# Output projection in two sets of banks, a fixed queue for the second norm, attention outputs scaled once per pair of heads

## The chip, the cores and the metric

The kernel runs on one core of a Trainium2 chip. The metric is device time in microseconds (us) of one execution. TensorE multiplies matrices, VectorE and ScalarE work element by element, GpSimd (POOL) does small operations and issues some DMAs, SyncE (SP) issues most of the others.

## The reference, cut to what matters

One layer over 1,024 frames of width 1,024: a norm, an input projection, two attentions (A in a band of chunks, B over keys that a top-k search selects), a gated recurrence C, a sigmoid-gated merge of the three, an output projection added to x, a second norm, a SwiGLU FFN added to x.

```python
h = rms_norm(x, g_mix[l])
z = h @ w_in[l]
...
p = jax.nn.softmax(sc, axis=-1).astype(v.dtype)
o = jnp.einsum('bhcqk,bckhd->bcqhd', p, vb)
...
merged = (gates[:, :, 0] * (y_a @ wb[:A_WIDTH])
          + gates[:, :, 1] * (y_b @ wb[A_WIDTH:A_WIDTH + B_WIDTH])
          + gates[:, :, 2] * (y_c @ wb[A_WIDTH + B_WIDTH:]))
x = x + merged @ w_out[l]
gu = rms_norm(x, g_ffn[l]) @ w_ffn_in[l]
g_, u_ = jnp.split(gu, 2, axis=-1)
x = x + (jax.nn.silu(g_) * u_) @ w_ffn_out[l]
```

## The kernel before

Every large product is made of three passes (`mm3`, L116 to L119): each operand is split into a high half, made by ScalarE (L101), and a low half, the rest, made by VectorE (L102), and high x high, high x low and low x high are added up in one bank of PSUM. The large products also go by a scheme with seven products of quarter matrices instead of eight, so that sums and differences of quarters have to be formed on VectorE before the splits and the results added after.

Instructions of each engine run in a fixed order. It is made when the program is built: a planner with a model of the durations takes, for each engine, the instruction that is ready by its model and stands first in the program. Loads on SP that are marked stay in program order. Buffers are slots of an arena with first-in first-out lists (`Slots`, L55); an instruction that writes a slot waits for the last reader of what was in it.

The stages, in the order of time: input norm and index scores (to some 90 us), then a long mixed stretch to some 620 us, in which the string `ORDER` (L38) interleaves the steps of attention A, the top-k search K, the gates G, C, attention B and others; the gates' rest to 670 us; the merge of the three branches to 788 us (L950 to L983); the output projection (L1081 to L1105); the second norm and the first FFN product (L1106 to L1110, L1217 to L1219); the FFN input part to some 1,310 us, the FFN output part to the end.

Attention (L396): for a pair of heads `pr`, a block `i` of 128 queries and each head `e`, `dots` puts scores into a bank S, L406 subtracts the maximum (VectorE), L409 takes the exp with its sum (ScalarE), L411 takes the reciprocal of the sum and L412 scales P (both VectorE), L418 transposes P (TensorE), L419 copies it back (ScalarE); L426 multiplies by v for both heads, L428 copies the result to 128 columns of `yT`. After the eighth block the pair's `yT` is stored to DRAM (L446 for A, L749 for B); it is loaded again in the merge.

Output projection (L958 to L1105): the merged M is kept in quarters; A11, A12, A21, A22 are quarters of M (two tiles each), b11 to b22 quarters of the weights, loaded by `load_wo` (b22 and b21 last). `o_prep(n)` forms the operands of product n and splits them; `order` (L1071) says which product comes when: 1, 5, 6, 4, 7, 2, 3. Each has four row tiles t of 12 matmuls of 512 columns, 48 in all. Products 1, 6 and 7 pile up in the banks X (0 to 3), the others have banks 4 to 7. `adds` (L1069) says into which half rows h and half columns of x2 each is added, with which sign (L1099).

Second norm (L993): for each of four row tiles a square with its sum (L997, ScalarE), a reciprocal root on POOL (L126, L127), a scaling (L999, VectorE), and a store of x2 (L1000). `evac2` transposes (L1016) and copies out (L1017). The norm of the upper rows and its splits (`trans2_first`) come after product 7, two products before the end; that of the lower rows after the last. Then `trans2_second` (L1032) forms the differences of quarters (L1039 to L1042) and splits them. `ffn_first(j)` makes two products of 12 matmuls with the quarters 11 and 21 of the upper rows alone; `ffn_rest(j)` makes the other five and needs T2, T1, T3, 22 and T4, in this order.

Of the kernel before, what the change touches and what calls it, by code (L numbers as in the profile page):

```python
# [10 lines left out]
F32 = mybir.dt.float32  # L11
# [68 lines left out]
def hybrid_kernel(ctx: ExitStack, tc: tile.TileContext, x, xt, small, cs, bias_a, lru_w, w_idx, w_zg, w_c, w_g, w_b,  # L80
# [315 lines left out]
    def attention(i, b0, pr, qk, v, mask, yT, isB=False):  # L396
# [4 lines left out]
        for e in range(2):  # L401
# [28 lines left out]

    def steps_A():
        for pr in range(2):
# [5 lines left out]
            yA = sl.get((128, T), F32, "yA")  # L438
            qk = to_stack(zA[pr], ga8, smc("ga", 1))
            for i in range(NT):  # L440
                b0 = max(0, i - 4)
                w = (i + 1 - b0) * 128
                attention(i, b0, pr, qk, vA, lambda h: bA[h % 2][:, 640 - w:640], yA)
# [296 lines left out]
    def steps_B():  # L740
        for pr in range(2):
            yB = sl.get((128, T), F32, "yB")
            qk = to_stack(zB[pr], None, None)
            for i in range(NT):
                w = (i + 1) * 128
                mk = mask[i] if i >= 2 else m01[:, 256 - w:256]
                attention(i, 0, pr, qk, vB, lambda h: mk, yB, True)
                if i == NT - 1:
                    nc.gpsimd.dma_start(y_dram[2 + pr], yB)  # L749
# [200 lines left out]
    for ot in range(8):  # L950
# [42 lines left out]
    def norm2(g):  # L993
        xn = []
        for t in range(4 * g, 4 * g + 4):
# [3 lines left out]
            V.tensor_scalar(j, x2[t], rs2[:, t:t + 1], None, op0=OP.mult)  # L999
# [20 lines left out]
    def keep(name, g, raw):  # L1020
        hb_[name, g] = (sl.get((128, 2, 512), F32R, "hh"), sl.get((128, 2, 512), F32R, "hl"))
        split(raw, *hb_[name, g])
# [8 lines left out]

    def trans2_second(xn, raws):  # L1032
        pairs = [(evac2(xn, g), evac2(xn, 2 + g)) for g in range(2)]
        sl.free(*xn)
        for g in range(2):
            b11, b21 = raws[g], raws[2 + g]
            b12, b22 = pairs[g]
            t2 = sl.get((128, 2, 512), F32, "t2")
            V.tensor_sub(b11, b12, b11)  # L1039
            V.tensor_tensor(b12, b22, b12, op=OP.subtract)  # L1040
            V.tensor_sub(t2, b22, b11)
            V.tensor_tensor(b21, b21, t2, op=OP.subtract)  # L1042
            for name, r in (("T2", t2), ("T3", b12), ("T1", b11), ("22", b22), ("T4", b21)):
                keep(name, g, r)
                sl.free(r)

    b22, b21 = load_wo(3), load_wo(2)
    A12, A21, A22 = ([M[kp + d][h] for kp in range(2)] for h, d in ((1, 2), (0, 0), (0, 2)))
    ss = [sl.get((128, 2, 512), F32, "s") for _ in range(2)]

    def o_prep(n):
        if n == "5":
            comb(ss, A21, OP.add, A22)
        elif n == "6":
            comb(ts, b22, OP.subtract, ts)
            comb(ss, ss, OP.subtract, A11)
        elif n == "4":
            comb(ts, ts, OP.subtract, b21)
# [3 lines left out]
        elif n == "3":  # L1062
            comb(ss, A12, OP.subtract, ss)
        r = o_split(*{"5": (ss, ts), "6": (ss, ts), "4": (A22, ts), "7": (A21, b12), "2": (A12, b21), "3": (ss, b22)}[n])
        for f in {"4": (A22, ts), "7": (A11, A21, b12), "3": (A12, ss, b21, b22)}.get(n, ()):
# [15 lines left out]
    for s_, n in enumerate(order):  # L1081
# [393 lines left out]
```

## Time and profile before

| | us |
|---|---|
| median of 3 runs | 1525.81 (1522.98 to 1526.56) |
| the profiled execution | 1523.58 |
| its span, first to last instruction | 1521.8 |
| TensorE busy | 1468.5 |
| VectorE busy | 1127.9 |
| ScalarE busy | 760.0 |

A busy share is an average over stages with different limits. Matmuls are pipelined, so each shows a duration of about 0.39 us while they start 0.23 us apart; the count of matmuls in a stretch says more than the busy time. PEclk is the clock granted to TensorE as a share of its full 2.4 GHz. A bracket at the end of an instruction's row gives the idle time of its engine before it and what ended that.

### The profile page before, as it was taken

To read this page: it belongs to the slowest core of one execution; us is meant where nothing else is said; L and a number is where in the kernel's file an instruction comes from. 1 tells how busy PE (TensorE), PEld (TensorE's weight loads), DVE (VectorE), ACT (ScalarE), POOL (GpSimd) and SP (SyncE) were. 2 spreads that over 40 slices of the span, in tenths; PEclk is the share of its full clock that TensorE was granted. 3 is DMA by queue.
4 is the path that set the end of the run, shared out by engine and by line. 5 is a ranking of instruction groups with operands and counts; after the bars stand their busy time and mean duration, and the time that the engine had idled before them with its cause. 6 is when DMAs were issued, how large, how long until landed. Compare 5 with 4: busy or idle time off the path is not lost.

```text
span 1521.8 us, 19934 instructions
## 1 busy us (share of the span) xinstructions
PE 1468.5 (96%) x7556; PEld 1227.0 (81%) x7556; DVE 1127.9 (74%) x1997; ACT 760.0 (50%) x1204; POOL 109.3 (7%) x161
## 2 busy tenths in 40 slices
PE   6999899999999998999998989999999999999999
PEld 5897688989788886788886868888888888888887
DVE  7889999869666779767889785555555556478872
ACT  6557768865778666443114563333333333344440
POOL 2220011210000200110000200000000000000000
PEclk9999999999999999999999999999999999999999
DMA  7011213112111121448461322323232323597532
GB/s 287 28 46 56 83 32 111 31 68 84 56 56 42 59 95 42 139 166 332 179 209 55 124 83 98 111 97 111 97 111 98 111 97 125 220 387 265 192 124 90
DMA packets 52241, 182.59 MB, mean 120 GB/s; under 512 B 6001, under 2 KB 6129, under 8 KB 52145
## 3 DMA queue, kind: packets, MB, share of 16 engines
q1 hardware_dynamic: 38448, 135.17, 25.8%
q0 software_dynamic: 11968, 43.00, 7.2%
q10 hardware_dynamic: 1728, 3.15, 0.5%
q8 instruction: 59, 0.97, 0.3%
q14 instruction: 38, 0.30, 0.1%
HBM read 135.94 MB, written 45.35 MB: 119 GB/s over the span
## 4 chain that ended last, share of the span: by engine, by line
PE 76%; DVE 17%; ACT 4%; issue 2%; DMA 1%; ACTq 0%; DVEq 0%; SPq 0%
PE B L119 15%; PE B L118 15%; PE B L117 14%; PE G L119 7%; PE G L118 7%; PE G L117 7%; DVE key L643 3%; PE T L426 2%; PE T L118 1%; PE T L119 1%; PE T L117 1%; PE T L418 1%; PE S L242 1%; PE S L117 1%; DVE ol L102 1%
## 5 line engine op out<-in xcount | busy, mean ns | idle before, releaser
L118 PE MATMUL B<-hl,fwh 128*128 128x512 f32 x528 | 205.1, 391 | 3.6 <-DVE hl L102 3.6
L117 PE MATMUL B<-hh,fwh 128*128 128x512 f32 x528 | 202.6, 391 | 3.3 <-ACT hh L101 3.3
L119 PE MATMUL B<-hh,fwl 128*128 128x512 f32 x528 | 198.2, 390 | 0.0
L117 PEld LDWEIGHTS B<-hh,fwh 128*128 128x128 f32 x528 | 99.5, 189 | 25.0 <-ACT hh L101 4.2
L118 PEld LDWEIGHTS B<-hl,fwh 128*128 128x128 f32 x528 | 99.6, 189 | 24.9 <-DVE hl L102 4.3
L118 PE MATMUL G<-wzl,hTh 128*128 128x256 f32 x384 | 110.8, 289 | 5.8 <-DVE wzl L102 5.7
L119 PEld LDWEIGHTS B<-hh,fwl 128*128 128x128 f32 x528 | 99.4, 188 | 20.6
L117 PE MATMUL G<-wzh,hTh 128*128 128x256 f32 x384 | 109.5, 287 | 2.3 <-ACT wzh L101 1.6
L102 DVE TENSOR_TENSOR fwl<-s,fwh 128x1024 fp32r<-128x1024 f32 x44 | 53.9, 1224 | 77.5 <-PE B L118 76.8
L119 PE MATMUL G<-wzh,hTl 128*128 128x256 f32 x384 | 110.1, 287 | 0.0
L118 PE MATMUL B<-fol,foh 128*128 128x512 f32 x264 | 102.7, 389 | 0.0
L119 PE MATMUL B<-foh,fol 128*128 128x512 f32 x264 | 101.9, 389 | 0.0
L117 PE MATMUL B<-foh,foh 128*128 128x512 f32 x264 | 101.1, 389 | 0.0
L655 ACT ACTIVATE junk_s<-score,ngS 128x1024 int8<-128x1024 f32 (+2 forms) x78 | 77.5, 993 | 17.7 <-DVE ngS L653 13.6
L118 PEld LDWEIGHTS G<-wzl,hTh 128*128 128x128 f32 x384 | 73.9, 192 | 7.7 <-DVE wzl L102 6.7
L119 PE MATMUL G<-hTh,wgl 128*128 128x512 f32 x192 | 76.0, 396 | 2.0 <-DVE wgl L102 2.0
L117 PEld LDWEIGHTS G<-wzh,hTh 128*128 128x128 f32 x384 | 73.6, 193 | 4.1 <-ACT wzh L101 2.0
L117 PE MATMUL G<-hTh,wgh 128*128 128x512 f32 x192 | 76.2, 397 | 0.0
L118 PE MATMUL G<-hTl,wgh 128*128 128x512 f32 x192 | 75.6, 394 | 0.0
L101 ACT ACTIVATE fw<-fb 128x512 fp32r<-128x512 f32 x22 | 14.0, 634 | 121.4 <-PE B L119 120.5
L119 PEld LDWEIGHTS G<-wzh,hTl 128*128 128x128 f32 x384 | 74.0, 193 | 0.4 <-issue 0.2
L1182 DVE TENSOR_TENSOR act<-act,B 128x512 f32<-128x512 f32 x22 | 15.1, 687 | 65.5 <-PE B L119 65.5
(486 smaller groups left out, 3872.7 us busy)
## 6 DMA issues: line engine op xcount, KB each, us to landing
fw<-in_w_fo SPq DMA_DIRECT2D x33, 512.0 KB, 5.7
fa<-pd SPq DMA_DIRECT2D x33, 512.0 KB, 5.5
gl<-gd SPq DMA_DIRECT2D x24, 512.0 KB, 5.5
fa<-in_w_fi SPq DMA_DIRECT2D x22, 512.0 KB, 3.5
fb<-in_w_fi SPq DMA_DIRECT2D x22, 512.0 KB, 3.5
pd<-act POOLq DMA_DIRECT2D x22, 512.0 KB, 5.3
ga<-in_w_g SPq DMA_DIRECT2D x18, 512.0 KB, 3.6
x<-in_x SPq DMA_DIRECT2D x16, 512.0 KB, 6.6
```

The lines of the kernel that those rows point to most:

```text
L101: S.activation(hi, raw, AF.Copy)
L102: (eng or V).tensor_tensor(lo, raw, hi.bitcast(F32), op=OP.subtract)
L117: PE.matmul(o, lhsT=lh, rhs=rh, start=first, stop=False, **kw)
L118: PE.matmul(o, lhsT=lh, rhs=rl, start=False, stop=False, **kw)
L119: PE.matmul(o, lhsT=ll, rhs=rh, start=False, stop=last, **kw)
L242: PE.matmul(sb[:, o + c0:o + c1], lhsT=q, rhs=kh[:, k0 + c0:k0 + c1], start=True, stop=False)
L418: PE.transpose(pt[:, b - c0], P[:, 128 * b:128 * b + 128], ident)
L426: PE.matmul(o[64 * e:64 * e + 64, :], lhsT=v[(b0 + b) // 4][:, (b0 + b) % 4, h, :], rhs=PT[e][:, b, :], start=b == 0, stop=b == nb - 1, sk ...
L643: V.tensor_scalar(o[:, 0:(i + 1) * 128], (keys or score)[i], ap[:, j:j + 1], 0.0, op0=op, op1=OP.add, accum_out=self.cnt[:, j:j + 1])
L655: S.activation(junk_s[:, 0:(i + 1) * 128], score[i], AF.Sign, bias=self.ng.bitcast(F32)[:, j:j + 1], accum_out=self.cnt[:, j:j + 1])
L1182: V.tensor_add(a1, a1, x)
```

## The change

- Attention: P is no longer scaled. The exp's sums of a pair go to columns of one tile, and after the pair's last block `normalise` takes their reciprocals, writes them to DRAM, brings them back as two broadcasts over 64 partitions each (one per head), and multiplies `yT` once before its store.
- Output projection: the order is 1, 5, 3, 6, 2, 7, 4; products 1, 6, 7, 4 share banks 0 to 3 and products 5 and 3 share banks 4 to 7; every product is followed by one addition per row tile; the halves of M change roles; product 3 has an operand tile of its own.
- Second norm: the scaling is done by ScalarE; the transposes of the upper rows use banks 4 to 7; VectorE's differences and splits of the lower rows are put in a fixed order (T2 of both groups, T1, T3, 22, T4), and the high halves are issued by `keep` itself; three `ffn_first` instead of two precede the first `ffn_rest`.

```diff
-            sm_ = const.tile([128, 1], F32, name="sum", bufs=4)
-            S.activation(P[:, 0:w], P[:, 0:w], AF.Exp, bias=nm, scale=-1.0, accum_out=sm_)
-            rc = const.tile([128, 1], F32, name="rc", bufs=4)
-            V.reciprocal(rc, sm_)
-            V.tensor_scalar(P[:, 0:w], P[:, 0:w], rc, None, op0=OP.mult)
+            S.activation(P[:, 0:w], P[:, 0:w], AF.Exp, bias=nm, scale=-1.0, accum_out=sums[:, e, i:i + 1])
...
+    rc_dram = [dram.tile([2, NT, 128], F32, name=f"rcd{n}") for n in range(4)]
+    def normalise(n, yT, sums):
+        rc = const.tile([128, 2, NT], F32, name="rc", bufs=2)
+        V.reciprocal(rc, sums)
+        nc.gpsimd.dma_start(rc_dram[n].rearrange("e i p -> p e i"), rc)
+        nT = sl.get((128, T), F32, "nT")
+        for e, half in enumerate((LO, HI)):
+            nc.gpsimd.dma_start(nT[half], rc_dram[n][e:e + 1].rearrange("e i p -> e (i p)").to_broadcast([64, T]))
+        V.tensor_mul(yT, yT, nT)
+        sl.free(nT)
...
                 if i == NT - 1:
                     sl.free(*bA)
+                    normalise(pr, yA, sums)
                     nc.gpsimd.dma_start(y_dram[pr], yA)
...
-            A11 = [M[kp][1] for kp in range(2)]
+            A11 = [M[kp][0] for kp in range(2)]
...
-            V.tensor_scalar(j, x2[t], rs2[:, t:t + 1], None, op0=OP.mult)
+            S.activation(j, x2[t], AF.Copy, scale=rs2[:, t:t + 1])
...
-            p = bank((128, 4, 128), (at + k) % 4) if at is not None else ybank((128, 4, 128))
+            p = ybank((128, 4, 128)) if at is None else bank((128, 4, 128), 4 + (at + k) % 4)
...
     def trans2_second(xn, raws):
         pairs = [(evac2(xn, g), evac2(xn, 2 + g)) for g in range(2)]
         sl.free(*xn)
+        yield
+        last = []
+
+        def step(f, *a):
+            if not last:
+                last.append(f(*a))
+                return
+            with tc.issue_after(last[0].ins):
+                last[0] = f(*a)
+
+        t2 = [sl.get((128, 2, 512), F32, "t2") for _ in range(2)]
+        for g in range(2):
+            step(V.tensor_sub, raws[g], pairs[g][0], raws[g])
+            step(V.tensor_sub, t2[g], pairs[g][1], raws[g])
+        for g in range(2):
+            step(keep, "T2", g, t2[g])
+        yield
+        for g in range(2):
+            step(keep, "T1", g, raws[g])
+            sl.free(raws[g])
...
-    A12, A21, A22 = ([M[kp + d][h] for kp in range(2)] for h, d in ((1, 2), (0, 0), (0, 2)))
-    ss = [sl.get((128, 2, 512), F32, "s") for _ in range(2)]
+    A12, A21, A22 = ([M[kp + d][h] for kp in range(2)] for h, d in ((0, 2), (1, 0), (1, 2)))
+    ss, s4_ = ([sl.get((128, 2, 512), F32, "s") for _ in range(2)] for _ in range(2))
...
+        elif n == "3":
+            comb(ss, ss, OP.subtract, A11)
+            comb(s4_, A12, OP.subtract, ss)
         elif n == "6":
             comb(ts, b22, OP.subtract, ts)
-            comb(ss, ss, OP.subtract, A11)
...
-    adds = {"1": ((1, 0, 1),), "5": ((1, 1, 1), (0, 1, 1)), "6": ((1, 1, 1),), "4": ((0, 0, -1),),
-            "7": ((0, 0, 1), (0, 1, 1)), "2": ((1, 0, 1),), "3": ((1, 1, 1),)}
-    order = "1564723"
+    adds = {"1": (0, 0), "5": (1, 1), "3": (0, 1), "6": (0, 1), "2": (0, 0), "7": (1, 1), "4": (1, 0)}
+    order = "1536274"
...
-            if n in "167":
-                p = X[t]
-            else:
-                p = bank(at=4 + t)
+            if n == "5" and t == 0:
+                Y = [bank(at=4 + u) for u in range(4)]
+            p = X[t] if n in "1674" else Y[t] if n in "53" else bank(at=4 + t)
...
-    for n in range(2):
+    for n, _ in enumerate(trans2_second(xn, raws2)):
         ffn_first(seq[n])
-    trans2_second(xn, raws2)
     for n in range(NF):
         ffn_rest(seq[n])
-        if n + 2 < NF:
+        if 0 < n and n + 2 < NF:
             ffn_first(seq[n + 2])
```

## Rows read from the trace of the kernel before

**Rows 1.** The page's first part: each engine's busy us, share, instructions.

```profile
PE 1468.5 (96%) x7556; PEld 1227.0 (81%) x7556; DVE 1127.9 (74%) x1997; ACT 760.0 (50%) x1204; POOL 109.3 (7%) x161
```

**Rows 2.** Busy time by stretch: its length, then each engine's busy us and count.

```profile
core 0: us, PE busy (x) PEld busy (x) DVE busy (x) ACT busy (x) POOL busy (x), PEclk, DMA share, GB/s
...
120.00:200.00 80.00, 71.09 (x376) 56.88 (x375) 78.53 (x279) 57.54 (x120) 2.22 (x4) 0.96 0.17 60
200.00:560.00 360.00, 354.54 (x2212) 302.07 (x2211) 278.51 (x590) 257.04 (x443) 36.60 (x37) 1.00 0.19 64
560.00:620.00 60.00, 54.35 (x355) 41.17 (x353) 56.47 (x90) 38.35 (x70) 1.62 (x3) 1.00 0.21 69
...
780.00:840.00 60.00, 53.96 (x227) 43.20 (x226) 56.04 (x62) 20.18 (x20) 0.00 (x0) 0.97 0.30 105
...
880.00:920.00 40.00, 33.06 (x151) 26.26 (x150) 33.22 (x35) 25.25 (x33) 0.00 (x0) 0.96 0.14 44
920.00:1500.00 580.00, 580.00 (x2560) 480.28 (x2559) 371.84 (x483) 212.99 (x272) 20.82 (x39) 1.00 0.42 151
```

**Rows 3.** Timeline of TensorE at four stretches: start, us, instruction, idle before.

```profile
165.11 0.50 PE L119 MATMUL G<-hTh,wgl 128*128 128x512 f32 x1 [2.03 <-DVE wgl L102]
...
814.03 0.50 PE L118 MATMUL B<-ol,oh 128*128 128x512 f32 x1 [2.85 <-DVE ol L102]
...
909.37 0.50 PE L118 MATMUL B<-hl,fwh 128*128 128x512 f32 x1 [2.93 <-DVE hl L102]
...
911.32 0.63 PE L118 MATMUL B<-hl,fwh 128*128 128x512 f32 x1
911.75 0.63 PE L119 MATMUL B<-hh,fwl 128*128 128x512 f32 x1
```

**Rows 4.** Groups by line, VectorE: busy us, mean ns, idle before and its releaser.

```profile
L412 DVE TENSOR_SCALAR P<-P,rc 128x640 f32<-128x640 f32 (+7 forms) x64 | 31.0, 491 | 0.6
...
L411 DVE RECIPROCAL rc<-sum 128x1 f32<-128x1 f32 x64 | 9.8, 157 | 7.8 <-ACT P L409 7.5
```

**Rows 5.** Busy time by stretch, VectorE's instructions of L412 alone.

```profile
120.00:200.00 80.00, 6.32 (x14) 0.96 0.17 60
...
560.00:600.00 40.00, 6.06 (x10) 1.00 0.19 59
```

**Rows 6.** DMA issues by line: engine, count, KB each, us from issue to landing.

```profile
yd<-yA POOLq DMA_DIRECT2D x2, 512.0 KB, 3.4
...
out_y<-xr SPq DMA_DIRECT2D x4, 256.0 KB, 2.0
...
s4d<-s POOLq DMA_DIRECT2D x1, 256.0 KB, 12.3
```

**Rows 7.** Groups by line, shapes apart, VectorE and ScalarE.

```profile
L1099 DVE SCALAR_TENSOR_TENSOR x<-B,x 128x512 f32<-128x512 f32 x36 | 23.4, 680 | 7.3 <-PE B L119 7.2
...
L102 DVE TENSOR_TENSOR hl<-h2r,hh 128x1024 fp32r<-128x1024 f32 x12 | 14.3, 1217 | 0.6 <-ACT hh L101 0.6
...
L999 DVE TENSOR_SCALAR xn<-x,rs 128x1024 f32<-128x1024 f32 x8 | 6.0, 749 | 1.1 <-POOL rs L127 1.0
...
L997 ACT ACTIVATE xn<-x 128x1024 f32<-128x1024 f32 x8 | 8.5, 1067 | 18.0 <-DVE x L1099 18.0
```

**Rows 8.** Timeline of VectorE in the output projection: operands of product 6.

```profile
802.43 1.21 DVE L939 TENSOR_TENSOR t<-wo,t 128x1024 f32<-128x1024 f32 x1
...
812.78 1.20 DVE L102 TENSOR_TENSOR ol<-t,oh 128x1024 fp32r<-128x1024 f32 x1
```

**Rows 9.** Timeline of VectorE after the second norm: first difference, last split.

```profile
889.38 1.23 DVE L1039 TENSOR_TENSOR h2r<-h2r,h2r 128x1024 f32<-128x1024 f32 x1 [0.60 <-ACT h2r L1017]
...
909.83 1.22 DVE L102 TENSOR_TENSOR hl<-h2r,hh 128x1024 fp32r<-128x1024 f32 x1
```

**Rows 10.** Timelines of POOL and SP: the last pair's store, the loads of y.

```profile
596.96 0.53 POOL L749 DMA_DIRECT2D yd<-yB  x1 [32.10 <-ACT yB L428]
...
672.29 16.90 SPq L107 DMA_DIRECT2D yr<-yd  x4
```

More of the change, by code (lines that the diff above doesn't have):

```diff
@@ L394, in steps_zA, with attention @@
         yield
-    def attention(i, b0, pr, qk, v, mask, yT, isB=False):
+    def attention(i, b0, pr, qk, v, mask, yT, sums):
         nb = i + 1 - b0
@@ L437, in steps_A @@
                 bA.append(bt)
-            yA = sl.get((128, T), F32, "yA")
+            yA, sums = sl.get((128, T), F32, "yA"), pair_sums()
             qk = to_stack(zA[pr], ga8, smc("ga", 1))
@@ L442, in steps_A @@
                 w = (i + 1 - b0) * 128
-                attention(i, b0, pr, qk, vA, lambda h: bA[h % 2][:, 640 - w:640], yA)
+                attention(i, b0, pr, qk, vA, lambda h: bA[h % 2][:, 640 - w:640], yA, sums)
                 if i == NT - 1:
                     sl.free(*bA)
+                    normalise(pr, yA, sums)
                     nc.gpsimd.dma_start(y_dram[pr], yA)
@@ L741, in steps_B @@
         for pr in range(2):
-            yB = sl.get((128, T), F32, "yB")
+            yB, sums = sl.get((128, T), F32, "yB"), pair_sums()
             qk = to_stack(zB[pr], None, None)
@@ L746, in steps_B @@
                 mk = mask[i] if i >= 2 else m01[:, 256 - w:256]
-                attention(i, 0, pr, qk, vB, lambda h: mk, yB, True)
+                attention(i, 0, pr, qk, vB, lambda h: mk, yB, sums)
                 if i == NT - 1:
+                    normalise(2 + pr, yB, sums)
                     nc.gpsimd.dma_start(y_dram[2 + pr], yB)
@@ L1034, in trans2_second @@
         sl.free(*xn)
-        for g in range(2):
-            b11, b21 = raws[g], raws[2 + g]
-            b12, b22 = pairs[g]
[L1038 to L1045, printed above, removed]
+        yield
[7 more added lines that the diff above has]
+        t2 = [sl.get((128, 2, 512), F32, "t2") for _ in range(2)]
+        for g in range(2):
+            step(V.tensor_sub, raws[g], pairs[g][0], raws[g])
[7 more added lines that the diff above has]
+        for g in range(2):
+            b12, b22 = pairs[g]
+            step(V.tensor_sub, b12, b22, b12)
+            step(keep, "T3", g, b12)
+            sl.free(b12)
+        for g in range(2):
+            step(keep, "22", g, pairs[g][1])
+            sl.free(pairs[g][1])
+        for g in range(2):
+            step(V.tensor_sub, raws[2 + g], raws[2 + g], t2[g])
+            step(keep, "T4", g, raws[2 + g])
+            sl.free(raws[2 + g], t2[g])
+        yield
     b22, b21 = load_wo(3), load_wo(2)
-    A12, A21, A22 = ([M[kp + d][h] for kp in range(2)] for h, d in ((1, 2), (0, 0), (0, 2)))
-    ss = [sl.get((128, 2, 512), F32, "s") for _ in range(2)]
+    A12, A21, A22 = ([M[kp + d][h] for kp in range(2)] for h, d in ((0, 2), (1, 0), (1, 2)))
+    ss, s4_ = ([sl.get((128, 2, 512), F32, "s") for _ in range(2)] for _ in range(2))
     def o_prep(n):
@@ L1094, in hybrid_kernel @@
                 (ah, al), (wh, wl) = cur[k // 2], cur[2 + k // 2]
-                mm3(p, ah[:, k % 2, c], al[:, k % 2, c], wh[:, k % 2], wl[:, k % 2], k == 0 and n not in "67", k == 3,
+                mm3(p, ah[:, k % 2, c], al[:, k % 2, c], wh[:, k % 2], wl[:, k % 2], k == 0 and n in "152", k == 3,
                     skip_group_check=True)
-            for h, ch, sign in adds[n]:
-                xs = x2[4 * h + t][:, 512 * ch:512 * ch + 512]
-                V.scalar_tensor_tensor(xs, p, 0.5 * sign, xs, op0=OP.mult, op1=OP.add)
+            h, ch = adds[n]
+            xs = x2[4 * h + t][:, 512 * ch:512 * ch + 512]
+            V.scalar_tensor_tensor(xs, p, 0.5, xs, op0=OP.mult, op1=OP.add)
         for i, q in enumerate(cur):
             (ring if i > 1 else sl).free(*q)
-        if n == "7":
+        if n == "2":
             xn = norm2(0)
```

16 lines of the change are left out of this document (9 added, 7 removed).

## The prediction

> **What bounds the kernel now.** I read the page's busy shares first, then the busy time by stage, then TensorE's own waits. TensorE is busy 96% of the span, so a microsecond is worth something only where TensorE stands still or runs slow [rows 1]. The change adds and removes no matmul: seven products of 48 matmuls in the output projection, the same transposes, the same products of the FFN. So its worth can hardly exceed what TensorE loses now, stage by stage. From 920 to 1500 us 2,560 matmuls took 580 us with no idle time: 0.2266 us each is full rate, and nothing can be won there [rows 2]. Elsewhere I count as lost the idle part of a stretch plus (1 - granted clock) times its length [rows 2]: 120 to 200 us 8.9 + 3.2 = 12.1 us; 200 to 560 us 5.5; 560 to 620 us 5.6; 780 to 840 us 6.0 + 1.8 = 7.8; 880 to 920 us 6.9 + 1.6 = 8.5. Together 39.5 us; the rest of the idle time is the start and the last stores, which the change doesn't touch.
>
> The releasers of the long gaps are low halves of a split, all made on VectorE: wgl at 165 us, ol at 814 us, hl at 909 us [rows 3]. After such a gap matmuls start 0.43 us apart instead of 0.2266 (911.32 to 911.75): the granted clock is at its lower level, 1.2 GHz, for some of them [rows 3]. VectorE is busy 78.5 of 80 us, 56.5 of 60 and 56.0 of 60 in the first, third and fourth of these stretches [rows 2]. The bound there is VectorE's queue, and the change takes work from it.
>
> **Attention.** Out go 64 reciprocals of 0.157 us and 64 scalings of 0.49 us on average, 9.8 + 31.0 = 40.8 us of VectorE [rows 4]. Of that, 14 pairs lie in 120 to 200 us: 6.3 + 14 x 0.157 = 8.5 us; ten in 560 to 600 us: 6.1 + 1.6 = 7.6 us; the other 40 pairs, 24.7 us, between them [rows 5].
> - 120 to 200 us: up to 8.5 us of the 12.1 could come back. But the planner will fill the freed time with rounds of the top-k search that are ready, and the late weights also wait for ring slots and ScalarE's high half. Between 0 and 8.5 I take 5.
> - 560 to 620 us: the last steps of B run as a chain exp, reciprocal, scaling, transpose; two links go, and the 7.6 us let the T step's sums start earlier. The cap is the 5.6 us that TensorE loses; I take 4, bounds 0 and 5.6.
> - 200 to 560 us: TensorE is covered; of 5.5 us I take 1, bounds 0 and 5.
>
> In come, four times, a reciprocal of 128x16 and a product of 128x1024, the latter like the 1.22 us of a split [rows 7]: at most 6 us of VectorE, against 40.8. The exps keep their accumulator reads. Between the two stands a round trip that the trace doesn't show: 16 pieces of 4 bytes from each of 128 partitions to DRAM, then two broadcasts of 256 KB back, all on POOL's queue. No reader of the result is hurried: y is loaded from 672 us, the last pair is stored at 597 [rows 10], and a late yT takes a buffer, not the path. What can hurt is order: the product waits at the head of VectorE's queue if the planner places it before the broadcast has landed, with splits, exps' inputs and top-k rounds behind it; POOL's reads wait for the write, with gate stores and the rsqrt of the next heads behind them. The trip's low end is two of the quickest landings, 2 x 2.0 = 4 us; its high end is two of the slowest, 2 x 12.3 us, plus an issue 16 times the 0.53 us of a 128-row store, 8.5 us: 33 us [rows 6, 10]. Being pure addition, it can't be a gain. I take 4 to 8 us, near the plain stores of 3.4 us [rows 6], mostly planned for, and charge 0.5 us a pair: 2 us; bounds 0 and 36 (9 us a pair).
>
> The Trainium skill, DMA: Bandwidth & Descriptors, Anatomy of one DMA, gives 2.0 us plus bytes over 436 GB/s for such a transfer; by it the trip would be an estimated 4.6 us, and the sum below would stand. The Rules for kernel authors on the same page speak against the change: a strided last dimension becomes one descriptor for each element. What that does here is the third rival.
>
> **Output projection.** More of the sums into x2 are now formed in the banks: products 1, 6, 7, 4 pile up in the first four banks, 5 and 3 in the other four. The 36 additions of 0.68 us become 28 [rows 7], 5.4 us less, but only 4 of these 8 (2.7 us) fall in the first four products, where the queue is late. The number of operand sums stays at 14. Third comes product 3 instead of 6, and it needs b22 as loaded, where 6 needed b22 minus a sum: in the trace that subtraction stands at 802.43, and its low half, which frees TensorE at 814.03, not before 812.78, with other products' operations in between [rows 8, 3]. One operation of 1.2 us less stands before that split. Cost: product 5 now reads the half of M finished last, two additions or 1.4 us later; product 1 covers this with 48 x 0.2266 = 10.9 us, and without cover it would cost 1.4. Gain: 2.7 + 1.2 of queue, and with it most of the slow clock; of the 7.8 us lost I take 5, bounds 0 and 7.8.
>
> **Second norm.** In both norms the scaling of xn goes from VectorE (0.75 us) to ScalarE (a pass there takes 1.07 us) [rows 7]: 8 x 0.75 = 6 us off VectorE, 0.3 us onto the chain from the last x2 to the transposes. The transposes' banks move to the half that is free; the same number of evacuations remain. Then the queue: today the first difference runs at 889.38, and the 18 differences and splits (8 and 10, 1.2 us each) end with the one at 909.83 [rows 9]. They are late because TensorE takes two first FFN products ahead of the transposes, and are made group by group, though the FFN wants T2 of both groups first. Now a third first product (24 x 0.2266 = 5.4 us) covers the wait, and the order is T2, T1, T3, 22, T4. If the transposes run when xn is ready, the first difference comes near 883, T2 near 890, T4 by 904, or 912 with some 9 us of weight splits between. TensorE, fed by three products, the transposes and four products of 12 matmuls, 2.7 us each, wants T2 at 897 and T4 at 908. So at most some 3 us of wait are left; without the early transposes only the 5.4 us of cover count. Of 8.5 us I take 7.5, bounds 4 and 8.5. The fixed order can hold a ready split behind an unready one, and three held weights use the last load buffers for the first round; both cost nothing while the third product covers them, and up to 3 us if not.
>
> **Sum.** 5 + 4 + 1 - 2 + 5 + 7.5 = 20.5 us. The profiled execution took 1523.58 us (span 1521.8), so 1503.1 us; the median of the three runs is 2.2 us above that execution, so 1505 us.
>
> **Rivals.**
> - The attention part pays nothing: top-k rounds take the freed time, and its waits move to the next split. For it: VectorE stays the busiest engine there after losing a tenth of its work. Against it: both long gaps wait for VectorE itself [rows 3]. Only 5 + 7.5 - 2 = 10.5 us remain: 1515 us.
> - The change doesn't do what it says: the planner reorders every queue once the costs change, and new waits take the place of the old; or the banks' reuse holds the transposes. The gains of some stages are eaten in others: 1525 us. For it: in 780 to 840 us VectorE never rested and yet had the low half wait ten us behind other work [rows 2, 8].
> - Slower: the product of `normalise` blocks VectorE until the broadcast lands, at the two ends of A above all, where VectorE is full. The gains without it are 22.5 us, so it decides from 22.5 / 4 = 5.6 us of TensorE loss per pair. With a trip in the upper half of the bounds, a late placement and 9 us lost per pair, 36 - 22.5 = 13.5 us are added: 1539 us. For it: an order planned for a short trip isn't corrected on the chip. Against it: a trip of 4 us costs nothing of the kind.
> - More than forecast: all 39.5 us less the few of switching, some 35 us: 1491 us.
>
> **How the numbers follow.** Forecast (1496 to 1512) 0.52; attention pays nothing 0.20; no change 0.10; slower 0.12; more 0.06. The range reaches over all but the slower case and the far edge of the best: 1491 to 1528 us. About 0.3%, 4.6 us, is what a measurement of this kernel can tell from no change. Faster 0.52 + 0.20 + 0.06 = 0.78; within 0.10; slower 0.12.
>
> **What would show it.** Right: no matmul gap over 2 us and a granted clock of 1.00 in the stretches that answer to 780 to 840 and 880 to 920; T2's splits adjacent, before T1's; some 35 us less VectorE time in all up to 620 us. Wrong: a VectorE idle time of several us before the new product, released by a DMA; a POOL issue of many us for the small pieces; gaps on low halves at 120 to 200 us as large as before; TensorE waiting for hh on ScalarE near the second norm. The forecast fails if the planner's order, not VectorE's amount of work, made the gaps.

## The result and the profile after

The changed kernel takes 1534.4 us (1532.3 to 1535.7) where the one before takes 1525.7 in the runs beside it: ratio 1.0060, 95% interval 1.0044 to 1.0076. It is some 9 us slower; I had forecast 1505. The profiled execution took 1533.39 us, its span is 1531.6, against 1523.58 and 1521.8. One execution among all the runs below, of 1603 us, fell in a slower state of the chip and is left out of its median.

The busy times first (page, first part: busy us, share, instructions), then those by stretch (length, then busy us and count of TensorE's matmuls, its weight loads, VectorE, ScalarE and POOL, then granted clock, DMA share, GB/s):

```profile
PE 1474.7 (96%) x7556; PEld 1231.2 (80%) x7556; DVE 1095.6 (72%) x1861; ACT 766.1 (50%) x1212; POOL 116.7 (8%) x173
```

```profile
120.00:200.00 80.00, 72.01 (x370) 56.53 (x369) 77.36 (x259) 57.73 (x119) 3.33 (x6) 0.94 0.20 68
200.00:560.00 360.00, 346.02 (x2162) 295.87 (x2161) 256.41 (x495) 250.83 (x431) 40.28 (x43) 0.99 0.20 62
560.00:620.00 60.00, 54.79 (x353) 42.54 (x352) 43.31 (x68) 35.79 (x75) 3.86 (x6) 0.94 0.26 80
780.00:840.00 60.00, 58.82 (x258) 47.79 (x257) 54.64 (x63) 20.15 (x20) 0.00 (x0) 1.00 0.44 158
880.00:920.00 40.00, 35.34 (x162) 26.79 (x160) 27.88 (x31) 29.12 (x39) 5.83 (x11) 1.00 0.22 79
920.00:1500.00 580.00, 576.97 (x2538) 477.62 (x2539) 379.66 (x490) 216.76 (x278) 20.84 (x39) 1.00 0.42 148
```

VectorE is busy 32.3 us less over the whole span; in 120 to 620 us, for which I had forecast some 35, the rows show 36.4 less (413.5 to 377.1) [rows 2], with the work itself some us behind. TensorE has the same 7,556 matmuls, but in 200 to 560 us it now stands idle for 14.0 us instead of 5.5 [rows 2], and in 120 to 200 and 560 to 620 the granted clock is lower (0.94) than before. The projection (780 to 840) is as good as forecast: 1.2 us idle and a full clock, where 6.0 us idle and 0.97 stood.

For all that follows I add up TensorE's lost time by stretch: from each matmul's start to the next, less the distance at which matmuls of its width follow each other undisturbed (0.2267 us for 512 columns). It takes in idle time and half clock alike. Stretches are by time; the work in them shifts by up to 13 us between kernels.

| lost us | 120-200 | 200-320 | 320-400 | 400-560 | 560-640 | 780-840 | 840-940 |
|---|---|---|---|---|---|---|---|
| before | 18.8 | 9.6 | 9.1 | 12.9 | 15.5 | 8.9 | 13.3 |
| changed | 19.5 | 15.8 | 14.0 | 11.8 | 19.5 | 2.0 | 15.3 |
| difference | +0.7 | +6.3 | +4.9 | -1.1 | +4.0 | -6.8 | +2.0 |

The differences sum to 10.0 us; the spans differ by 9.8. So the attention stretches lost 15 us instead of giving 8, the projection gave 7, and the second norm took 2.

**Where the attention stretches lost it.** The DMA issues of the new trip (line, queue, count, KB each, us from issue to landing):

```profile
nT<-rcd POOLq DMA_DIRECT2D x8, 256.0 KB, 4.7
rcd<-rc POOLq DMA_DIRECT2D x4, 8.0 KB, 10.8
```

The write of 8 KB takes 10.8 us to land; the 256 KB reads behind it 4.7. The first trip, 206.06 to some 223, is about 17 us (the four take 17 to 19), where I had guessed 4 to 8. The product of L441 doesn't wait for it at VectorE's head. Two others pay. The timeline of POOL at the first trip, and VectorE's row that waits for it (start, us, instruction, idle before and what ended it):

```profile
206.06 1.19 POOL L437 DMA_DIRECT2D rcd<-rc  x1 [12.64 <-DVE ngS L667]
217.41 1.05 POOL L440 DMA_DIRECT2D nT<-rcd  x2 [10.15 <-issue]
218.53 0.20 POOL L126 TENSOR_SCALAR rs_v<-s 128x16 f32<-128x16 f32 x1
218.82 2.94 POOL L127 TENSOR_TENSOR r<-rs_v,mhalf 128x16 f32<-128x16 f32 x1
```

```profile
221.78 1.23 DVE L347 TENSOR_TENSOR zA<-zA,r 128x1024 f32<-128x1024 f32 x1 [4.69 <-POOL r L127]
```

The reads stand on POOL's queue until the write has landed, and the next heads' reciprocal root (L126, L127) stands behind the reads; VectorE idles 4.69 us for it. TensorE's longest wait in this stretch comes some 30 us later, for the high half of a weight:

```profile
253.15 0.50 PE L117 MATMUL G<-hTh,wgh 128*128 128x512 f32 x1 [2.33 <-ACT wgh L101]
```

The second trip, on POOL, SP, ScalarE and TensorE:

```profile
328.29 1.17 POOL L437 DMA_DIRECT2D rcd<-rc  x1 [5.65 <-DVE rc L436]
341.20 1.06 POOL L440 DMA_DIRECT2D nT<-rcd  x2 [11.74 <-issue]
```

```profile
333.92 0.33 SPq L107 DMA_DIRECT2D wcxr<-in_w_c  x1
```

```profile
345.18 1.06 ACT L101 ACTIVATE wcxh<-wcxr 128x1024 fp32r<-128x1024 f32 x1 [10.40 <-DMA wcxr<-in_w_c]
346.14 0.26 ACT L424 ACTIVATE yA<-T 128x128 f32<-128x128 f32 x1
```

```profile
346.45 1.81 PE L414 MATMUL T<-ident,P 128*128 128x128 f32 x6 [7.23 <-ACT yA L424]
```

The four loads of this weight, 512 KB each, in the changed kernel:

```profile
DMA to landing us min/median/max: 3.5/3.6/11.2
```

The one issued at 333.92, while the write is under way, takes 11.2 us; the median is 3.6. Its split stands at ScalarE's head and waits 10.40 us, the copy of yA behind it comes late, and TensorE, which wants its bank, stands 7.23 us. Nobody in this chain uses the reciprocals.

**Where the second norm lost it.** ScalarE, VectorE and TensorE after the transposes (hh and hl are the high and low halves of the FFN's input, fwh and fwl those of its weights; t is T2, h2r the other quarters):

```profile
900.40 1.11 ACT L1037 ACTIVATE hh<-t 128x1024 fp32r<-128x1024 f32 x1
...
903.25 1.10 ACT L1037 ACTIVATE hh<-h2r 128x1024 fp32r<-128x1024 f32 x1
904.36 1.28 ACT L1254 ACT_TABLE_LOAD   x1
...
906.19 1.04 ACT L1037 ACTIVATE hh<-t 128x1024 fp32r<-128x1024 f32 x1
```

```profile
907.27 1.22 DVE L1038 TENSOR_TENSOR hl<-t,hh 128x1024 fp32r<-128x1024 f32 x1 [2.61 <-ACT hh L1037]
908.41 2.35 DVE L1038 TENSOR_TENSOR hl<-h2r,hh 128x1024 fp32r<-128x1024 f32 x2
```

```profile
923.03 0.50 PE L119 MATMUL B<-hh,fwl 128*128 128x512 f32 x1 [3.10 <-DVE fwl L102]
```

VectorE's queue is fixed, ScalarE's is not. The planner put two other high halves, a weight's, a table load and a gate between T2's first high half (900.40) and its second (906.19). VectorE holds still at its head for 2.61 us, with T1's two splits behind it, although T1's high halves were ready. Behind that TensorE stands 3.10 us at 923 for the low half of a weight that is late.

### The profile page after: what moved, and what is told of

Read it like the earlier page. It is cut to its first block, busy times and chain, and to the rows that moved or that the text cites. A ratio compares the mean times of both kernels' runs of the same rounds, so it can differ in the third digit from the quotient of the medians.

```text
span 1531.6 us, 19824 instructions
## 1 busy us (share of the span) xinstructions
PE 1474.7 (96%) x7556; PEld 1231.2 (80%) x7556; DVE 1095.6 (72%) x1861; ACT 766.1 (50%) x1212; POOL 116.7 (8%) x173
## 2 busy tenths in 40 slices
DMA packets 53072, 184.71 MB, mean 121 GB/s; under 512 B 6321, under 2 KB 6449, under 8 KB 52977
## 4 chain that ended last, share of the span: by engine, by line
PE 61%; ACT 3%; DVE 2%; DMA 1%; issue 1%; ACTq 0%; DVEq 0%
PE B L119 15%; PE B L118 14%; PE B L117 14%; PE G L119 3%; PE G L117 3%; PE G L118 3%; PE T L118 1%; PE T L117 1%; PE T L119 1%; PE S L117 1%; PE S L118 1%; PE S L119 1%; PE T L422 1%; PE T L414 1%; DVE hl L1038 1%
## 5 line engine op out<-in xcount | busy, mean ns | idle before, releaser
L101 ACT ACTIVATE foh<-fa 128x1024 fp32r<-128x1024 f32 x33 | 35.0, 1060 | 57.7 <-DMA fa<-pd 49.0
```

The source lines that it names most:

```text
L101: S.activation(hi, raw, AF.Copy)
```

## The experiments

Each measured time is the median, the ratio is against the kernel before on the same chip, with its 95% interval. The runs lie on four chips, so differences between runs are given by ratios, or by medians where both agree within about a microsecond.

### The attention part, taken apart

**Attention part alone.** Edit: the attention hunks of the diff on the kernel before, nothing else.

> The kernel before with the attention part of the change alone (unscaled P, sums of a pair kept, one reciprocal, the trip through DRAM, one product per pair); projection and second norm as before. Theory A (the trip's small-piece writes, and what they delay, cost more than the VectorE work taken off brings): about 1535 to 1542, slower than before by 10 to 16, since the changed kernel lost about 15 us more of TensorE time in its attention stretches and got back 7 in the projection. Rival B (the attention part by itself gives what I forecast, 8 to 10, and the loss comes from its meeting with the other parts): about 1516. Rival C (the attention part is worth nothing either way): within 3 of before.

Measured: 1536.8, ratio 1.0075 (1.0063 to 1.0087). Theory A: this part by itself costs 11.5 us.

**Without the normalise step.**

```diff
-                    normalise(pr, yA, sums)
...
-                    normalise(2 + pr, yB, sums)
```

> As the run with the attention part alone, but normalise is left out altogether: no reciprocal, no DMA, no product, so the attention outputs stay unscaled. It times what the taken-off VectorE work (the 128 reciprocals and scalings, some 41 us of VectorE) is worth by itself. If my forecast's +10 for the attention loop was right and only the trip spoilt it: about 1515. If the VectorE work was never on the path that sets TensorE's pace: 1523 to 1528, no change, and then the trip costs some 12. If taking it off makes things worse by itself (other work gets ahead on VectorE and ScalarE and the weight splits come late): over 1529.

Measured: 1520.3, 0.9961 (0.9948 to 0.9974). Taking off the 41 us of VectorE work, with the order that the planner makes for it, is worth 6 us, not 10; the normalise step costs 17. The windows of this run:

```profile
120.00:200.00 80.00, 71.48 (x359) 55.90 (x358) 77.26 (x258) 57.63 (x119) 2.78 (x5) 0.94 0.19 64
200.00:560.00 360.00, 357.72 (x2245) 306.28 (x2245) 259.71 (x506) 259.20 (x450) 35.77 (x36) 1.00 0.19 63
560.00:620.00 60.00, 54.84 (x352) 42.22 (x351) 51.66 (x70) 38.61 (x69) 2.71 (x5) 0.97 0.24 79
```

In 120 to 200 us VectorE is as full as before (77.3 against 78.5 [rows 2]): work from further on has moved up. In 560 to 620 it got 4.8 us of free room, and TensorE gained 0.5 us of busy time and lost clock. The gain is in 200 to 560, where I had put 1 us: 2.3 us idle instead of 5.5.

**The same bytes in larger pieces.** Edit, on the attention part alone:

```diff
-        nc.gpsimd.dma_start(rc_dram[n].rearrange("e i p -> p e i"), rc)
+        nc.gpsimd.dma_start(rc_dram[n].rearrange("e i p -> (e i p)").rearrange("(p k) -> p k", k=16),
+                            rc.rearrange("p e i -> p (e i)"))
```

> The attention part alone, and in it one thing changed: each of the four writes of the reciprocals puts 128 pieces of 64 bytes into DRAM (in another order, so the factors that come back belong to other queries: the turn of the table is left out) instead of 2048 pieces of 4 bytes. Every engine's order of instructions is the same as in the attention part alone, so that only the piece size differs. Theory A (the small pieces hold up the loads that run beside them): the write lands in about 2 us instead of 11.8, the weight load beside the second one in under 5 us instead of 11, the gap of TensorE near 346 (5 us and the half clock after it) goes, and the time falls by 5 to 9 below 1538, to 1529 to 1533. Rival (another order of the engines is the cause): within 2 of 1538, gap still there.

Measured: 1525.7, 0.9997 (0.9988 to 1.0006). This is the cleanest pair of the study: all engines run the same instructions in the same order, the same 8 KB goes out, and 0.78%, 11.9 us, are gone. The write and TensorE's longest wait in 320 to 400 us in the attention part alone:

```profile
rcd<-rc POOLq DMA_DIRECT2D x4, 8.0 KB, 11.8
```

```profile
345.87 1.82 PE L414 MATMUL T<-ident,P 128*128 128x128 f32 x6 [4.99 <-ACT yA L424]
```

With larger pieces, its DMA issues, the four loads of the weight, and TensorE's longest wait in 320 to 400 us (waiter, releaser: us in total, times, longest):

```profile
wcxr<-in_w_c SPq DMA_DIRECT2D x4, 512.0 KB, 4.0
rcd<-rc POOLq DMA_DIRECT2D x4, 8.0 KB, 1.7
```

```profile
DMA to landing us min/median/max: 3.6/4.0/4.3
```

```profile
PE T L422 <- ACT PT L415: 0.6, 1, 0.6
```

1.7 us to land instead of 11.8, and the 5 us gap is gone. In lost time: 200 to 320 fell from 15.6 to 11.0, 320 to 400 from 12.4 to 6.3.

**The changed kernel itself with larger pieces.** The same edit on the changed kernel, again with every engine's order kept.

> The changed kernel itself, with the four writes of the reciprocals in 128 pieces of 64 bytes instead of 2048 of 4 bytes (left out: the turn of the table, so the factors belong to other queries). Every engine's order of instructions is that of the changed kernel. If the piece size costs in the changed kernel what it costs with the attention part alone (1538 to 1526, 12): 1522 to 1524, and the 7.2 us gap at 346 and that at 253 go. If the other parts had changed its price: anywhere from 1526 to 1534.

Measured: 1519.8, 0.9958 (0.9946 to 0.9970), 14.6 us below the changed kernel. Its windows:

```profile
200.00:560.00 360.00, 355.27 (x2226) 303.43 (x2225) 264.38 (x511) 257.24 (x444) 39.92 (x44) 1.00 0.20 67
560.00:620.00 60.00, 53.06 (x351) 40.30 (x350) 49.70 (x69) 38.54 (x71) 3.22 (x6) 1.00 0.23 74
```

4.7 us idle in 200 to 560 where 14.0 stood. By stretch: 5.0 back in 200 to 320, 7.4 in 320 to 400, 2.7 in 560 to 640. The waits shown above are gone with it: the reciprocal root starts at 215.59 us instead of 218.53, VectorE's row behind it follows without a wait, and TensorE has no gap over 1 us in 200 to 560. The piece size alone turns the changed kernel from 9 us slower to 6 faster.

**Write alone, and write with reads, no product.**

```diff
         nc.gpsimd.dma_start(rc_dram[n].rearrange("e i p -> p e i"), rc)
-        nT = sl.get((128, T), F32, "nT")
...
-        V.tensor_mul(yT, yT, nT)
```

> The attention part alone with the reciprocals and their four writes in pieces of 4 bytes, but without the reads and the product (left out: the scaling). Nobody waits for these writes. Theory A (the small pieces by themselves hold up other loads): 5 to 9 above the run without the normalise step, 1525 to 1530. If they only matter because something waits for them: 1519 to 1522.

Measured: 1526.8, 1.0004 (0.9995 to 1.0013): 6.5 us above the kernel without normalise, for four reciprocals and four writes that nobody waits for. ScalarE's and SP's orders are the same in both. The lost time in 320 to 400 went from 5.1 to 10.6; ScalarE and TensorE there:

```profile
336.84 1.06 ACT L101 ACTIVATE wcxh<-wcxr 128x1024 fp32r<-128x1024 f32 x1 [4.98 <-DMA wcxr<-in_w_c]
```

```profile
338.12 0.48 PE L414 MATMUL T<-ident,P 128*128 128x128 f32 x1 [4.08 <-ACT PT L415]
```

And with the reads as well:

> The attention part alone with the writes in pieces of 4 bytes and the broadcast reads, but without the product (left out: the scaling). If the DMAs, writes and reads together, cost nearly all of the 18: 1533 to 1538, and the reads by themselves are the difference to the run with the writes only. If the product's place on VectorE (behind the trip) is a large part: 1525 to 1530.

Measured: 1540.7, 1.0096 (1.0081 to 1.0112), which is even above the attention part with its product (1.0075). So the product is not what costs here, as far as kernels with different orders can tell.

**Product without DMAs.**

```diff
-        nc.gpsimd.dma_start(rc_dram[n].rearrange("e i p -> p e i"), rc)
...
-        V.tensor_mul(yT, yT, nT)
+        V.tensor_mul(yT, yT, yT)
```

> The attention part alone without the trip: the reciprocals are taken, but nothing is written to DRAM or read back, and the product multiplies the pair's output by itself, so it keeps its place and size on VectorE. Left out: the scaling itself. With the normalise step left out altogether the time was 1520, with the whole of it 1538. If the trip's DMAs cost the 18: about 1521 to 1523 (four products of 1.2 us and four reciprocals, little of them on the path). If the product at the end of a pair is what costs: 1530 to 1538. If neither, the remaining order of the engines decides, and the time may lie anywhere between.

Measured: 1529.3, 1.0025 (1.0016 to 1.0033): 9 us above the kernel without normalise, with no DMA added, and 3.5 above the one with 64-byte writes, reads and product. I had no place for this. Four products and reciprocals are 6 us of VectorE, but TensorE lost 9 more in 320 to 400 alone. Its longest gap there, and that of the next experiment:

```profile
387.90 0.47 PE L541 MATMUL S<-us,lwh 128*128 128x512 f32 x1 [2.54 <-DVE us L213]
```

```profile
389.15 0.45 PE L414 MATMUL T<-ident,P 128*128 128x128 f32 x1 [2.85 <-DVE kl L229]
```

These gaps near 385 to 392 us, with a lower clock after them, have no like over 0.9 us in the kernel before, nor in the two with 64-byte pieces. The planner had made another order of TensorE's instructions, from 239 us on. The amount of VectorE's work alone isn't the cause: the attention part with 64-byte pieces has the same matmuls, the same number and sizes of instructions on VectorE and ScalarE, twelve DMAs more and another order, and no such gap. In the run with twice the scaling (below), whose order is new too, gaps of 1.73 and 2.08 us stand at 388 and 391 us. That the order is the cause is inferred, not shown: no run changed the order and nothing else.

**The table turned before the write.**

```diff
-        nc.gpsimd.dma_start(rc_dram[n].rearrange("e i p -> p e i"), rc)
+        pt = tbank((128, 4, 128))
+        PE.transpose(pt[0:16, 0], rc.rearrange("p e i -> p (e i)"), ident)
+        rT = const.tile([16, 128], F32, name="rT", bufs=1)
+        V.tensor_copy(rT, pt[0:16, 0])
+        nc.gpsimd.dma_start(rc_dram[n].rearrange("e i p -> (e i) p"), rT)
```

> As the run with the attention part alone, but the reciprocals are turned on TensorE (one [128,16] transpose into PSUM and a copy to a [16,128] tile) before they are written, so that the write to DRAM has 16 rows of 512 bytes instead of 2048 pieces of 4 bytes; reads, product and the rest as they were. Theory A (the small pieces hold up the other DMAs): the write lands in 2 to 3 us instead of 10.8, the 512 KB weight load behind it in 3 to 4 instead of 11.2, the 7.2 us gap of TensorE near 346 is gone, and the time is 5 to 10 below that of the attention part alone. Rival (the pieces are harmless; the loss is from moved work or the reads): within 2 of the attention part alone.

Measured: 1534.0, 1.0054 (1.0042 to 1.0066). The write lands in 1.6 us and the gap at 346 is gone, yet only 3 us came back: by lost time 5.1 us won in 200 to 320 and 8.1 in 320 to 360, then the gaps near 390, and 9.4 lost again in 360 to 400 (each against the attention part alone). Theory A fails in its time: the mend works, and something new takes most of it back.

**Twice the scaling.** On the kernel before:

```diff
             V.tensor_scalar(P[:, 0:w], P[:, 0:w], rc, None, op0=OP.mult)
+            V.tensor_scalar(P[:, 0:w], P[:, 0:w], 1.0, None, op0=OP.mult)
```

> The kernel before with each scaling of P followed by a second one by 1.0: 64 more instructions of 0.49 us, 31 us more of VectorE in the same places. If the amount of VectorE work sets TensorE's pace in the attention stretches, as I forecast (10 us back for 41 us taken off), 31 us more should cost some 8 or more: 1534 or later. If VectorE only has its free room there, and the waits come from chains and from the order: within 4 of before, as the reverse of the 0 to 6 that taking the scaling off brought.

Measured: 1536.1, 1.0069 (1.0057 to 1.0081), 10.6 us for 31 us more. Its windows:

```profile
120.00:200.00 80.00, 73.16 (x391) 57.97 (x391) 79.04 (x283) 54.44 (x111) 2.23 (x4) 0.98 0.19 67
200.00:560.00 360.00, 349.01 (x2170) 299.68 (x2169) 287.60 (x622) 254.94 (x434) 39.75 (x37) 0.98 0.18 62
560.00:620.00 60.00, 53.12 (x350) 40.72 (x350) 56.27 (x117) 37.35 (x80) 1.07 (x2) 0.97 0.16 55
```

In 120 to 200, the fullest stretch, it costs nothing: TensorE is even better off (lost 17.2 against 18.8). The cost falls in 320 to 400 (+5.2) and 560 to 640 (+6.8). So 31 us added cost 10.6 and 41 taken off give 6, and neither is paid where VectorE is fullest. Both kernels also have new orders (this one from 134 us on), so the two prices aren't those of the VectorE work alone.

### Projection and second norm

**Both, without the attention part.** Edit: all hunks of the diff but those of attention.

> The change without its attention part: before, with the projection's new order and banks and the second norm's fixed order and split stages. From the two traces the projection gave back 6.9 us of TensorE time and the second norm cost 2: so 1519 to 1522. Rival 1 (the second norm's two loss is an effect of what the attention part moved, or of the clock): 1513 to 1517. Rival 2 (the projection's gain is lost again later): 1524 to 1527.

Measured: 1520.3, 0.9964 (0.9952 to 0.9976). Up to 745 us, in the merge, every engine's order is that of before; the projection's stretch lost 2.0 us instead of 8.9, and 840 to 940 lost 13.6 instead of 13.3.

**Projection alone.** Edit: order, `adds`, `o_prep`, the banks and the halves of M.

> Before with the projection's part of the change alone (order of the products, banks, roles of the halves); second norm and attention as before. With the second norm's part the time is 1520.3. If the second norm's part is worth nothing, as the traces say (13.3 us of lost TensorE time in 840 to 940 before, 13.6 with it): 1519 to 1521.5. If it is worth the 7.5 that I forecast and the projection less: 1525 or more. If it costs: under 1519.

Measured: 1517.4, 0.9938 (0.9926 to 0.9950). The projection is worth 9 us, and the second norm's part costs 3 to 4 on top of it (0.9964 against 0.9938). In the trace 6.9 us of the 9 come back in 780 to 840, and some 2 in 840 to 940, where this kernel has the second norm of before.

**ScalarE's high halves in the same fixed order.** On projection and second norm:

```diff
-        S.activation(hb_[name, g][0], raw, AF.Copy)
+        if name in ("T2", "T1", "T3", "22", "T4"):
+            if ka_:
+                with tc.issue_after(ka_[0].ins):
+                    ka_[0] = S.activation(hb_[name, g][0], raw, AF.Copy)
+            else:
+                ka_.append(S.activation(hb_[name, g][0], raw, AF.Copy))
+        else:
+            S.activation(hb_[name, g][0], raw, AF.Copy)
```

> Projection and second norm of the change, without the attention part, and ScalarE's high halves of the lower rows put in the same fixed order as VectorE's differences (T2 of both groups, T1, T3, 22, T4). Theory A (VectorE's fixed queue waits 2.6 us at its head for T2's second high half, which ScalarE makes after halves of T1 and 22, a weight's, a table load and a gate): that wait falls under 1 us, and the time falls by 2 to 3 below 1520.3. Rival (the wait is covered, the next splits of weights are what TensorE waits for, or ScalarE gets a wait of its own at its head): within 1.5 of 1520.

Measured: 1515.6, 0.9925 (0.9912 to 0.9938). TensorE's waits in 870 to 940 us (us in total, times, longest), without the edit and with it:

```profile
PE B L119 <- DVE fwl L102: 3.1, 1, 3.1
PE B L117 <- ACT hh L1022: 2.1, 3, 0.8
PE B L118 <- DVE hl L1023: 1.6, 2, 0.9
PE B L117 <- ACT fwh L101: 0.5, 1, 0.5
```

```profile
PE B L118 <- DVE hl L1032: 1.5, 2, 1.3
PE B L117 <- ACT hh L1027: 0.8, 1, 0.8
PE B L119 <- DVE fwl L102: 0.7, 1, 0.7
```

7.3 us of waits became 3.0, and the time fell by 4.7 by the medians, 6.0 by the ratios. It has the lowest ratio of the study, 0.75% below the kernel before and, by the two ratios, 1.3% below the changed one.

**Three first products ahead.** The loop of three `ffn_first` before the call of `trans2_second`, its yields run through after.

> Projection and second norm of the change, without the attention part, but the three first FFN products are all issued ahead of the differences and splits of the lower rows, instead of one ahead, one between T2 and T1 and one behind T4 in program order. Theory A (the third one comes too late in TensorE's order to cover the wait for T2): TensorE has 24 more matmuls, 5.4 us, to run during that wait, and the time falls by 3 to 5 to about 1516. Rival (its own weight split then stands ahead of the differences on VectorE and ScalarE and makes T2 later): within 2 of 1520 or slower.

Measured: 1521.1, 0.9958 (0.9946 to 0.9970): no gain. With ScalarE's order as well:

> Projection and second norm of the change with ScalarE's high halves in the fixed order (1515.7), and all three first FFN products ahead of the differences. Without ScalarE's order the third product ahead gave nothing (1521 against 1520). If the waits for ScalarE hid its worth: 1512 to 1514. If its own weight split makes T2 later by as much as it covers: within 1.5 of 1515.7 or slower.

Measured: 1516.3, 0.9937 (0.9924 to 0.9949): the same as without. The cover that I had counted at 5.4 us is worth nothing in either case.

**The scaling back on VectorE**, without and with ScalarE's order:

```diff
-            S.activation(j, x2[t], AF.Copy, scale=rs2[:, t:t + 1])
+            V.tensor_scalar(j, x2[t], rs2[:, t:t + 1], None, op0=OP.mult)
```

> Projection and second norm of the change, without the attention part, but the scaling of xn stays on VectorE. Projection alone measured 1517.4, both parts 1520.3. If the move of the scaling to ScalarE (0.3 us longer each, on the chain from the last sum of squares to the transposes, in front of ScalarE's evacuations) costs the 3: 1516 to 1518. If the fixed order costs them: 1520 or later.

Measured: 1519.2, 0.9957 (0.9945 to 0.9969).

> Projection and second norm of the change with ScalarE's high halves in the fixed order (1515.7), but the scaling of xn on VectorE again. If the scaling's move to ScalarE costs once the order is mended (0.3 us each on the chain, ScalarE's evacuations behind it): 1513 to 1515. If it brings what I forecast, VectorE's 6 us before the differences: 1517 to 1519. If it is worth nothing either way: within 1.5 of 1515.7.

Measured: 1515.6, 0.9933 (0.9917 to 0.9949). The move of the scaling is worth nothing either way.

**VectorE's order left to the planner.**

```diff
-            with tc.issue_after(last[0].ins):
-                last[0] = f(*a)
+            last[0] = f(*a)
```

> Projection and second norm of the change, without the attention part, and the fixed order of VectorE's differences and splits of the lower rows left to the planner; three first products, split stages and the scaling on ScalarE as in the change. If the fixed order costs, by waiting 2.6 us at its head for T2's second high half: 1516 to 1518. If the order is worth something and only ScalarE's unordered halves spoil it: 1521 or later.

Measured: 1518.8, 0.9957 (0.9945 to 0.9970). By medians 1.5 us below the run with the fixed order, but within its interval. Which of the edits makes the 3 to 4 us of the second norm stays open; shown is that ScalarE's order gives them back. With it the second norm's part is some 2 us better than the projection alone (0.9925 against 0.9938), but the intervals overlap.

**The whole change with both mends**, the turned table and ScalarE's order.

> The whole change with two mends: the reciprocals are turned on TensorE and written in 16 rows of 512 bytes, and ScalarE's high halves of the lower rows are in the fixed order too. By the sum of the single results: changed kernel 1534, small pieces away 14.6 (from the run with 64-byte pieces), ScalarE's order 4.6: 1515 to 1516, if the planner places the turned table as well as it placed the write. With the attention part alone the turned table gave only 3 to 4 back, since TensorE's transpose and the order around it moved: then 1525 to 1527.

Measured: 1524.6, 0.9993 (0.9985 to 1.0002). The table's small pieces are gone and the second norm lost 12.0 us instead of 15.3, but the gaps near 390 are there again (12.4 lost in 320 to 400). With its arithmetic complete, the attention part has no version here that pays.

## Why the prediction was wrong

| step | forecast | measured | by |
|---|---|---|---|
| attention, VectorE work taken off | +10 | +6 | the run without normalise |
| normalise | -2 (bounds 0 to 36) | -17 | attention part with and without it |
| of it the piece size | | -12 | same order, 64-byte pieces |
| of it the rest | | -5 to -6 | 64-byte pieces against no normalise; work and order not separated |
| projection | +5 (0 to 7.8) | +9 | projection alone |
| second norm | +7.5 (4 to 8.5) | -3 to -4 | with and without it, projection in both |

The measured parts sum to some -5 or -6, the whole change measured -9; a gap of 3 us is no more than the intervals of the ratios leave open.

- **Normalise: the failing step.** The term that failed is the 2 us charged for the trip. I bounded the trip by rows of large transfers, from 2.0 to 12.3 us each, took 4 to 8 us because plain stores land in 3.4 [rows 6], and charged 0.5 us a pair. Those were the wrong rows: the cost went by pieces. The trip takes 17 us and costs 4 us a pair. I even had the sentence: a strided last dimension becomes one descriptor for each element (the Trainium skill, DMA: Bandwidth & Descriptors, Rules for kernel authors); this case agrees in time, 10.8 us against 1.7 for the same bytes. The estimate of 4.6 us for the trip, from Anatomy of one DMA on that page of the Trainium skill, doesn't hold: the trace has 17. I let that estimate and the stores outweigh the rule.
- **Who pays.** I looked for the cost at the product, at VectorE's head. In the changed kernel VectorE never waited for nT. The cost fell on two others: a load on another queue (11.2 us instead of 3.6), and the reciprocal root behind the reads on POOL's queue. The second I had named but given no price of its own; the first I hadn't thought of. A DMA was taken as hidden because no one waits for its result; it wasn't, because a load on another queue slowed down beside it, and in the run with the writes alone, too.
- **Attention's gain.** Forecast 5 in 120 to 200, 4 in 560 to 620, 1 in between; by lost time in the traces -2, 0 and 5 (the two profiled executions are 3.3 us apart, the medians 6). The rival that the freed time fills up was right for the first stretch. That gaps there end with a VectorE split [rows 3] doesn't say that VectorE's load makes them: taking 8.5 us of work off there raised TensorE's lost time by 2.0, adding 6.3 lowered it by 1.6, each with another order.
- **Projection: right in its mechanism, sized too small.** No half clock and no low-half wait of 2.85 us [rows 3] is left; the remaining gaps are 0.78 and 0.40 us. In its own stretch 6.9 us came back, inside the bounds; the 9 us of the run alone lie above them, since I had counted nothing behind 840 us.
- **Second norm: wrong in its premise.** I had the transposes run when xn is ready. The last xn was ready at 889.9, but TensorE ran matmuls of the first FFN products before and between the transposes, the first evacuation started at 893.9 and the first difference at 895.2, 10.9 us after the last addition instead of 13.1: 2.2 us where I had counted on some 6. Then I priced the fixed order at nothing "while the third product covers" it. The order was fixed on VectorE alone, and it became a wait for ScalarE's free one. TensorE waiting for hh on ScalarE near the second norm was in my list of what would show it wrong. The third product's cover, counted at 5.4 us, gave nothing in either run that issued it ahead of the differences.
- **The rivals.** The slower one (1539, 0.12) was the nearest in time; its trip, 17 to 19 us, came out in the middle of the bounds (4 to 33), its 9 us a pair were 4, and its blocked product was wrong. "The planner's order, not VectorE's amount of work" was right in part, as far as the runs tell: kernels whose work differs by 6 us of VectorE differ by 9 in time, with new gaps in places that the edit doesn't touch.

## What to carry to other kernels

Price a DMA by its pieces and by what else is in flight, not by its bytes or by who waits for it; if its layout forces pieces of an element, try first what the same bytes cost in whole rows, with the order of all engines kept. If the order of one engine is fixed by hand, fix that of the engine that feeds it as well, or the fixed queue inherits every accident of the free one. Before work is taken off a full engine, add some in the same place: what that costs the bound engine hints at the stretches in which the load matters at all, as far as the order stays the same.

## What the runs showed of the hardware that I hadn't expected

- 8 KB to DRAM in pieces of 4 bytes took 9.7 to 14.1 us to land in the four kernels that have them (medians 10.8 in the changed kernel, 11.8 in the attention part alone), in pieces of 64 bytes 1.7 and in 16 rows of 512 bytes 1.6 (medians). The issue on POOL took 1.18 us against 0.54. The count of packets on the page hardly differs (53,072 in the changed kernel, 53,007 with 64-byte pieces), so it doesn't show the pieces.
- While the small pieces were under way, a 512 KB load from another queue took 11.2 us (8.9 in the attention part alone, 8.5 beside the writes alone, 13.7 without the product) instead of 3.6; with 64-byte pieces none of this weight's loads took over 4.4.
